# Values of layer 1 for four pairs of heads in one job, with two of its four weight slabs in other tiles, and splits of late outputs placed behind the last transposed weights

## The chip, the cores and the metric

The kernel runs on one core of a Trainium2 chip. The metric is the device time of one execution in microseconds (us); lower is better. The program is one launch: TensorE (PE, with its weight loads as PEld), VectorE (DVE), ScalarE (ACT), GpSimd (POOL) and the DMA queue that SyncE (SP) feeds, each with its own instruction stream that is worked off in order.

## The reference

Two layers of an encoder trunk on 1024 tokens of width 1024, in f32. Every layer does

```
h = rms_norm(x) * (1 + scale(c)) + shift(c);  x = x + gate(c) * mixer(h)
```

and a last `rms_norm` follows. Layer 0's mixer is differential attention beside a bidirectional RG-LRU. Layer 1's mixer, which the change is about, is neighbourhood attention over a 16 x 64 grid:

```
q, k, v, g = split(h @ w_in, 4)                 # 16 heads of 64
p = softmax(q k^T / 8 + relative bias, masked)  # window 8 rows x 16 columns
y = ((p v) * silu(g)) @ w_out
```

## The kernel before, in words

All activations are kept transposed: a tile holds 128 of the 1024 features, and a half `hf` of the tokens (512). A weight matrix comes in slabs of 1024 x 128 (512 KB). `load_next` loads a slab into one of two `raw` tiles by SP's queue. `split_next` cuts it into a high part `whi` (ACT, L187) and a low part `wlo` (POOL, four instructions, L190), both in a format that TensorE multiplies fast. Activations are cut the same way into `ahi` and `alo`. Each product is then three matmuls, high x high, high x low and low x high (`mm3`, L206 to L208). `slab(i)` makes sure that slab i is split, and `ahead(i)` splits it early. Slabs are split in the order of the list `slabs`. The pool and the tags that `split_next` picks say which tile a slab goes into, and a split waits until the last matmul has read the slab that was there before.

`proj` multiplies one slab with half of the tokens: 24 matmuls with 512 columns into one bank of PSUM, then an evacuation, `evac_k`, `evac_q` or `evac_g`. The evacuation of a key (L641 to L644) puts the high part down by ACT (`ks`) and the low part by DVE.

Between layer 0's output and layer 1 lies a boundary stage. Layer 1's input is made from x by a norm: DVE works out the reciprocal root of the mean square in a chain of small instructions on tiles of 128 x 128 (`rstd_rows`, `rs`, `rr`, `rt`, L390 to L396), eight matmuls spread it over all partitions (`bc`, L409), and `make_h` (L416 to L418) makes x * gain * bc on DVE, `ahi` on ACT and `alo` on DVE, for each of eight tiles. The first half of the tokens goes through this while layer 0's second half is still being multiplied. For the second half the PE covers the norm with layer 1's first projections of the first half: k, q and g of pair 0.

Layer 1 works in pairs of heads p = 0 to 7 and 64 units u = 8p + 4hf + b. `na_a` makes a unit's logits (`n`, four matmuls, L673 and L674), DVE adds the bias and takes the maximum (L1383), ACT the exponential (L1386), POOL the division by the sum (L1391). `na_b` transposes the result (`etr`, six matmuls, L1402) and copies it out of PSUM by DVE (L1408) and ACT (L1406). `na_c` multiplies four units with the values (`no`, 48 matmuls, L1420). The PE's time between these is filled from a queue of projections, `Feed`: each step of a job is some six or twelve matmuls and has a price, mostly 1300 ns, and each unit gives a credit, `PUMP1` (4400 ns). `upto` finishes a job by force where a unit needs it.

Values are the one projection with the tokens as the stationary operand. `v1_job(p)` makes them for pairs p and p + 1 from two slabs, for each of eight groups of 128 tokens: 24 matmuls with 256 columns into a bank, then a copy `vt` by ACT or DVE, and a store to the DRAM tensor `vd`. `load_v` reads them back in the layout that `na_c` wants (`vch`).

What sets the order: Python writes the program in the order of these jobs, a scheduler then sorts each engine's instructions by priority and by its own estimate of when each can start, and `high_priority` and `issue_after` move single ones. The resulting order on each engine is fixed.

In layer 1's output stage `out_layer` first splits the eight mixed tiles for both halves (`split_act`, ACT L232 and DVE L233), then runs the output slabs over them in the order of features 6, 0, 1, 2, 3, 4, 5, 7. Pairs from `LATE` = 3 on are gated after their attention (`gate1`, L1319); the output of the last pair is `o_7`.

Of the kernel before, what the change touches and what calls it, by code (L numbers as in the profile page):

```python
# [19 lines left out]
P = 128  # L20
# [9 lines left out]
NW = (3, 3, 7, 3)  # L30
KORDER1 = (6, 0, 1, 2, 3, 4, 5, 7)
PUMP = 745.0
PUMP1 = 4400.0
LATE = 3

DA_HEADS = 4
LRU_CHUNKS = 4
# [60 lines left out]
def kernel(ctx, tc, xT, xTp, small, lamp, adaw, tb, w0, gw, wo0, w1, nab, wo1, out):  # L98
# [62 lines left out]
    def split_next():  # L161
        i = state["split"]
        if i >= len(slabs):
            return
        while state["load"] <= i:
            load_next()
        raw = raws.pop(i)
        pool = wp
        if state["third"] is not None:
            state["turn"] = (state["turn"] + 1) % 3  # L170
            pool = wp if state["turn"] else state["third"]
        tags = ("whi", "wlo")
        if i == 2:
            pool, tags = kqp, ("ks1", "ks1")
        if i == at1["g", 0]:
            pool, tags = mixp[1], ("mix6", "mix7")
        j = i - len(slabs) + KC
        if j >= 0:

            pool = (wp, kqp, mixa, mixp[1])[j // 2]  # L180
            if j >= 2:
                tags = (("ks0", "ks0"), ("ks1", "ks1"), ("mix0", "mix1"), ("mix2", "mix3"),
                        ("mix4", "mix5"), ("mix6", "mix7"))[j - 2]
        hi = pool.tile([P, KC, P], F32R, tag=tags[0], name=f"whi{i}")
        lo = pool.tile([P, KC, P], F32R, tag=tags[1], name=f"wlo{i}")
        with tc.high_priority() if j < 2 else tc.issue_after(state["pool"]):
            A.activation(hi[:], raw[:], AF.Copy)  # L187

            for k in range(0, KC, 2):
                G.tensor_tensor(lo[:, k:k + 2], raw[:, k:k + 2], hi[:, k:k + 2], ALU.subtract)  # L190
# [264 lines left out]
    for p in range(NA_PAIRS):  # L455
        vs = [("v", p), ("v", p + 1)] if p % 2 == 0 else []
        kq = [("k", p), ("q", p)]
        order1 += kq + vs if p else kq + [("g", 0)] + vs
        if 0 < p < LATE:
            order1.append(("g", p))  # L460
    order1 += [("g", p) for p in range(LATE, NA_PAIRS)]
    base1 = {"q": 0, "k": 8, "v": 16, "g": 24}
    for key in order1:
        at1[key] = len(slabs)
# [663 lines left out]
    def out_layer(l, ato, xsrc, xdst, pool, korder, order, view, segments):  # L1128
# [88 lines left out]
    with tc.tile_pool(name="bound", bufs=2) as bp:  # L1217
        make_sel(bp)
        run, tail = out_layer(0, ato0, xTp, x1d, bp, [4, 5, 6, 7, 0, 1, 2, 3], by_fours, by_tile,
                              ((0, 0, 0, HF), (KC, 1, 0, HF)))  # L1220
        r0, r1 = run(0), run(1)
        mod = mods(NM[2], bp, bufs=4, wait=NW[2])
        for c in range(KC):
            some(r0, 1)
            after_dve(mod, 3)

        t0 = tail(0, to_h1)
        for c in range(KC):
# [25 lines left out]
    with ExitStack() as l1:  # L1254
# [9 lines left out]
        def v1_job(p):  # L1264

            i = at1["v", p]
            ws = [slab(i), slab(i + 1)]
            for t in range(8):
                hf, b = divmod(t, 4)
                ps = bank("v1")  # L1270
                for k in range(KC):
                    hi, lo = (t[:, b * P:(b + 1) * P] for t in hact[k, hf])
                    wh, wl = (w[:].rearrange("p (k a) n -> p k (a n)", a=2)[:, k % 4, :]
                              for w in ws[k // 4])
# [3 lines left out]
                vt = ap.tile([P, 256], F32, tag="vt", name="vt", bufs=2)  # L1278
                if t % 2:
                    A.activation(vt[:], ps[:, :256], AF.Copy)  # L1280
                else:
                    V.tensor_copy(vt[:], ps[:, :256])
                state["vd"] = nc.sync.dma_start(
                    vd4[2 * hf:2 * hf + 2, 64 * b:64 * b + 64, P * p:P * p + 256], vt[:]).ins
                if t == 1:
                    ahead(i + 2)
                yield 1300.0

        def load_v(p, b):
# [9 lines left out]

        def load_ahead(p):  # L1300

            if f"1v{p + 1 - (p + 1) % 2}" in feed.done:
                for b in range(4):
                    load_v(p + 1, b)

# [14 lines left out]

        state["gate1"] = gate1
        feed.done.add("1g0")
        for p in range(NA_PAIRS):
            if p:
                feed.add(f"1k{p}", both(at1["k", p], evac_k(("b", p))))
                feed.add(f"1q{p}", both(at1["q", p], evac_q(("b", p))))
            if p % 2 == 0:
                feed.add(f"1v{p}", v1_job(p))
            if 0 < p < LATE:
                feed.add(f"1g{p}", both(at1["g", p], evac_g1l(p)))  # L1330
        for p in range(LATE, NA_PAIRS - 2):
            feed.add(f"1g{p}", both(at1["g", p], evac_g1l(p)))

        def last_gates():

# [59 lines left out]
        def na_b(u, e):  # L1395
# [41 lines left out]
        es, ets = {0: na_a(0)}, {}  # L1437
        for u in range(n_units + 1):

            pump = 1.5 * PUMP1 if u < 3 else PUMP1  # L1440
            if u and u % 4 == 0:
                na_c(u - 4, [ets.pop(u - 4 + b) for b in range(4)])
            if u % 8 == 2:

                p = u // 8
                feed.upto(f"1v{p - p % 2}")
                for b in range(4):
                    load_v(p, b)
            elif u >= 8:
# [51 lines left out]

def _slabs_v(w):

    n = w.shape[1] // 256
    return w.reshape(2, 4, P, n, 256).transpose(3, 0, 2, 1, 4).reshape(2 * n, P, KC, P)


def _t5_bucket(rel):
# [75 lines left out]
```

## Time and profile before

| what | value |
|---|---|
| median of 3 runs | 1181.23 us (1179.83 to 1182.94) |
| the profiled execution | 1183.27 us, of which the span is 1181.5 us |
| PE busy | 1142.2 us, 97% |
| DVE, ACT, POOL busy | 715.9, 559.5, 440.5 us (61%, 47%, 37%) |
| layer 1's units, first logits to last product with values | 618.1 to 1078.4 us |
| value matmuls | 768 with 256 columns |
| matmuls of projections with 512 columns, groups `pp<-ahi` and `pp<-alo` | 3 x 848 |

The page gives the busy time of each engine, the span in 40 slices, the DMA queues, the chain of waits that ended last, and the costliest groups of instructions. A matmul's duration reaches from its issue to its modelled end, and the next begins before that, so the cost of a matmul in a row of them is the distance between two starts. A row of a timeline gives start, duration, engine, line and operation, and in brackets how long the engine was idle before and what ended that.

### The profile page before, as it was taken

The page shows a single profiled execution, that of the slowest core. Times are in us where ns is not written, and L with a number is a line of the kernel's source. Part 1 is how long each engine was busy: PE and PEld are TensorE (multiplying, and loading weights), DVE is VectorE, ACT ScalarE, POOL GpSimd, SP SyncE. Part 2 cuts the span into 40 slices and gives each one's busy share as a digit, 9 for nine tenths or more (in the row PEclk, how much of TensorE's full clock was granted, in tenths as well). Part 3 has the DMA queues.
Part 4 walks back from the last instruction along what each step waited for, and adds up shares of the span by engine and source line. Part 5 has one row for each costly group of instructions (what it writes and reads, how often), then busy time and mean ns, then how long its engine had stood idle before and what let it go on. Part 6 is the DMA issues. An engine that isn't in the chain of part 4 may idle for free.

```text
span 1181.5 us, 19490 instructions
## 1 busy us (share of the span) xinstructions
PE 1142.2 (97%) x7232; PEld 974.7 (82%) x7232; DVE 715.9 (61%) x1422; ACT 559.5 (47%) x1029; POOL 440.5 (37%) x586
## 2 busy tenths in 40 slices
PE   4999999999999999999998999999999999999997
PEld 3788778888887888778788889988988998887896
DVE  6857968699889989768462344334444444454254
ACT  4357685476655557533332444344345444445121
POOL 3135445243343332456522444333243333417200
PEclk8999999999999999999999999999999999999999
DMA  9723141432122012484522533343453543314312
GB/s 330 239 72 123 47 140 56 141 90 79 37 86 64 32 39 72 156 296 173 181 79 91 145 106 98 91 135 110 127 162 99 153 138 106 95 34 149 106 73 72
DMA packets 85791, 136.48 MB, mean 116 GB/s; under 512 B 8000, under 2 KB 49472, under 8 KB 85696
## 3 DMA queue, kind: packets, MB, share of 16 engines
q1 hardware_dynamic: 85696, 135.23, 36.3%
q8 instruction: 57, 0.93, 0.3%
q14 instruction: 38, 0.31, 0.1%
HBM read 112.13 MB, written 16.78 MB: 109 GB/s over the span
## 4 chain that ended last, share of the span: by engine, by line
PE 76%; DVE 9%; DMA 6%; ACT 4%; POOL 2%; issue 1%; SPq 0%; DVEq 0%; ACTq 0%; POOLq 0%
PE pp L206 15%; PE pp L207 15%; PE pp L208 15%; PE no L1420 4%; PE etr L1402 3%; PE v L206 2%; PE v L208 2%; PE v L207 2%; POOL wlo L190 2%; PE atr L1035 2%; PE n L673 2%; DMA ada<-in_adaw_dram 2%; DVE e L1005 2%; PE n L674 2%; PE s L673 1%
## 5 line engine op out<-in xcount | busy, mean ns | idle before, releaser
L206 PE MATMUL pp<-ahi,whi 128*128 128x512 f32 (+1 forms) x976 | 370.1, 379 | 0.1
L207 PE MATMUL pp<-alo,whi 128*128 128x512 f32 (+1 forms) x976 | 368.1, 377 | 0.0
L208 PE MATMUL pp<-ahi,wlo 128*128 128x512 f32 (+1 forms) x976 | 367.6, 377 | 0.2 <-POOL wlo L190 0.2
L190 POOL TENSOR_TENSOR wlo<-raw,whi 128x256 fp32r<-128x256 f32 x320 | 264.3, 859 | 221.0 <-ACT whi L187 199.0
L208 PEld LDWEIGHTS pp<-ahi,wlo 128*128 128x128 f32 x976 | 183.7, 188 | 34.4 <-POOL wlo L190 0.6
L206 PEld LDWEIGHTS pp<-ahi,whi 128*128 128x128 f32 x976 | 183.8, 188 | 32.5 <-issue 0.9
L207 PEld LDWEIGHTS pp<-alo,whi 128*128 128x128 f32 x976 | 183.8, 188 | 30.5 <-issue 0.2
L1391 POOL TENSOR_SCALAR e<-e,r 128x288 f32<-128x288 f32 (+1 forms) x128 | 71.5, 572 | 224.9 <-DVE r L1389 224.8
L187 ACT ACTIVATE whi<-raw 128x1024 fp32r<-128x1024 f32 x80 | 84.3, 1056 | 109.0 <-PE pp L207 58.0
L1386 ACT ACTIVATE e<-e,nm 128x288 f32<-128x288 f32 (+1 forms) x128 | 72.7, 569 | 51.1 <-DVE nm L1383 43.8
L1009 ACT ACTIVATE e<-e,nm 128x1024 f32<-128x1024 f32 x64 | 73.6, 1150 | 46.6 <-DVE nm L1005 46.3
L1408 DVE COPY e<-etr 96x384 f32<-96x384 f32 (+1 forms) x64 | 35.5, 554 | 91.4 <-PE etr L1402 90.4
L1383 DVE CUSTOM_DVE_ANT_0 e<-n,bias 128x288 f32<-128x288 f32 (+1 forms) x128 | 60.5, 504 | 47.8 <-PE n L674 33.0
L1406 ACT ACTIVATE e<-etr 96x384 f32<-96x384 f32 (+1 forms) x64 | 31.3, 490 | 114.9 <-DVE e L1408 111.6
L1005 DVE CUSTOM_DVE_ANT_0 e<-s,tb 128x1024 f32<-128x1024 f32 x64 | 77.3, 1218 | 6.0 <-PE s L674 4.9
L1026 POOL TENSOR_SCALAR e<-e,r 128x256 f32<-128x256 f32 x32 | 33.5, 1046 | 124.4 <-DVE r L1015 76.0
L206 PE MATMUL v<-whi,ahi 128*128 128x256 f32 x256 | 72.8, 284 | 0.0
L208 PE MATMUL v<-whi,alo 128*128 128x256 f32 x256 | 72.5, 283 | 0.0
L207 PE MATMUL v<-wlo,ahi 128*128 128x256 f32 x256 | 72.4, 283 | 0.0
L1042 ACT ACTIVATE ath<-atr 128x512 fp32r<-128x512 f32 x64 | 37.5, 596 | 37.8 <-PE atr L1035 37.5
L1151 DVE SCALAR_TENSOR_TENSOR xh<-pp,mod,xh 128x512 f32<-128x512 f32 (+1 forms) x37 | 23.4, 634 | 49.9 <-PE pp L208 43.3
L1402 PE MATMUL etr<-ident,e 128*96 128x128 f32 (+1 forms) x384 | 52.3, 272 | 0.8 <-POOL e L1391 0.8
(218 smaller groups left out, 2117.0 us busy)
## 6 DMA issues: line engine op xcount, KB each, us to landing
raw<-in_w_dram SPq DMA_DIRECT2D x56, 512.0 KB
ada<-in_adaw_dram SPq DMA_DIRECT2D x96, 256.0 KB
raw<-in_wo_dram SPq DMA_DIRECT2D x24, 512.0 KB
bias<-in_nab_dram SPq DMA_DIRECT2D x64, 144.0 KB
qq<-qq SPq DMA_DIRECT2D x48, 128.0 KB
bias<-in_nab_dram SPq DMA_DIRECT2D x32, 192.0 KB
xT<-in_xT_dram SPq DMA_DIRECT2D x16, 256.0 KB
vd<-vt SPq DMA_DIRECT2D x32, 128.0 KB
```

The source lines that it names most:

```text
L187: A.activation(hi[:], raw[:], AF.Copy)
L190: G.tensor_tensor(lo[:, k:k + 2], raw[:, k:k + 2], hi[:, k:k + 2], ALU.subtract)
L206: T.matmul(ps, lh, rh, start=start, stop=False)
L207: T.matmul(ps, lh, rl, start=False, stop=False)
L208: state["pe"] = T.matmul(ps, ll, rh, start=False, stop=stop).ins
L1005: state["dve"] = V.tensor_tensor_reduce(out=e[:], in0=ps[:].rearrange("p a b -> p (a b)"), in1=tbt["tb"][:, o:o + S], scale=-1.0, scalar=3 ...
L1009: A.activation(e[:], e[:], AF.Exp, scale=-1.0, bias=nm[:], accum_out=sums[:, m:m + 1])
L1383: state["dve"] = V.tensor_tensor_reduce(out=e[:, m, :n], in0=ps[:, m, :n], in1=bias["now"][m][:, :n], scale=-1.0, scalar=3.0e38, op0=ALU.a ...
L1386: A.activation(e[:, m, :n], e[:, m, :n], AF.Exp, scale=-1.0, bias=nm[:, m:m + 1], accum_out=sums[:, m:m + 1])
L1391: state["pool"] = G.tensor_scalar(e[:, m, :n], e[:, m, :n], r[:, m:m + 1], 0.0, ALU.mult, ALU.add).ins
L1402: T.transpose(pt[:kn, m, j * P:(j + 1) * P], e[:, m, j * kn:(j + 1) * kn], ident[:])
L1420: T.matmul(po[64 * m:64 * m + 64, b * P:(b + 1) * P], vch[p, b][:kn, j + hf, 64 * m:64 * m + 64], ets[b][:kn, m, j * P:(j + 1) * P], start ...
```

## The change

It has five parts.

1. `v1_job` makes the values of four pairs at once from four slabs. A slab holds 256 of the features of h for 512 columns, and a group of tokens takes 24 matmuls with 512 columns. It pauses three times inside a group, not once, and copies a bank out in two pieces of 256 columns, one by DVE and one by ACT, each with its store. There are two such jobs, `v0` and `v4`, where there were four.
2. Homes: of the first job's slabs, the first two are split into the tiles of the later mixed outputs 4 and 5, and 2 and 3; of the second job's, the last two into those of 4 and 5, and 6 and 7.
3. All four slabs of the first job are split ahead in the boundary stage.
4. The order of jobs is written out in `JOBS1`. The credit of a unit is 5000 ns up to unit 30 and 3450 ns behind it, and doubled for unit 0.
5. The splits of the mixed tiles 3 and up in layer 1's output stage are placed behind DVE's last copy of transposed weights, and the modulation that layer 1's output needs is spread over the units from 17 on, not from 26.

```diff
-PUMP1 = 4400.0
+PUMP1 = (5000.0, 3450.0)
+JOBS1 = "k0 q0 g0 v0 k1 q1 g1 k2 q2 g2 k3 q3 v4 k4 q4 k5 q5 k6 q6 g3 k7 q7 g4 g5 g6 g7"
...
+        pool, tags = wp, ("whi", "wlo")
+        if i == 2:
+            pool, tags = kqp, ("ks1", "ks1")
+        elif i == at1["g", 0] or i == at1["v", 4] + 3:
+            pool, tags = mixp[1], ("mix6", "mix7")
+        elif i in (at1["v", 0], at1["v", 4] + 2):
+
+            pool, tags = mixp[1], ("mix4", "mix5")
+        elif i == at1["v", 0] + 1:
+            pool, tags = mixa, ("mix2", "mix3")
+        elif state["third"] is not None:
...
-                    split_act(k, hf, mixed[k][:, hf * HF:(hf + 1) * HF], V, order)
+
+                    with tc.issue_after(state["etr"]) if l and k >= LATE else nullcontext():
+                        split_act(k, hf, mixed[k][:, hf * HF:(hf + 1) * HF], V, order)
...
-        ahead(at1["g", 0] + 2)
+        for j in range(2, 5):
+            ahead(at1["g", 0] + j)
...
-            ws = [slab(i), slab(i + 1)]
+            ws = [slab(i + j) for j in range(4)]
...
-                for k in range(KC):
+                for n, k in enumerate(range(KC)):
...
-                    mm3(ps[:, :256], hi, lo, wh, wl, k == 0, k == KC - 1)
-                    if k == 3:
+                    mm3(ps, hi, lo, wh, wl, n == 0, n == KC - 1)
+                    if n % 2 == 1 and n < KC - 1:
                         yield 1300.0
...
+                for j in range(2):
+                    vt = ap.tile([P, 256], F32, tag="vt", name="vt", bufs=2)
+                    src, c0 = ps[:, 256 * j:256 * j + 256], P * p + 256 * j
+                    if j:
+                        A.activation(vt[:], src, AF.Copy)
+                    else:
+                        V.tensor_copy(vt[:], src)
+                    state["vd"] = nc.sync.dma_start(
+                        vd4[2 * hf:2 * hf + 2, 64 * b:64 * b + 64, c0:c0 + 256], vt[:]).ins
...
-                    V.tensor_copy(e[:kn, m, :], pt[:kn, m, :384])
+                    state["etr"] = V.tensor_copy(e[:kn, m, :], pt[:kn, m, :384]).ins
...
-            pump = 1.5 * PUMP1 if u < 3 else PUMP1
+            pump = PUMP1[u > 30] * (2.0 if u == 0 else 1.5 if u < 3 else 1.0)
...
-            if u >= 26:
+            if u >= 17:
```

The engines' orders are the same up to the boundary stage. There ACT's order changes. `whi_5828` and `whi_5769` are the slabs of g and q of pair 0, `ks_5803` and `ks_5804` the evacuation of its keys, `qq` that of its queries, `ahi_1` the second half of layer 1's input. Before:

```order
L187 ACTIVATE whi_5828<-raw_5767 128x1024
L187 ACTIVATE whi_5769<-raw_5728 128x1024
L1156 ACTIVATE sq<-xh_1_7_5689 128x512
L641 ACTIVATE ks_5803<-pp_0_5778 64x4x2x64
L642 ACTIVATE ks_5804<-pp_0_5778 64x4x2x64
L657 ACTIVATE qq_5862<-pp_0_5837 64x512
L658 ACTIVATE qq_5863<-pp_0_5837 64x512
L417 ACTIVATE ahi_1_5886<-xh_1_0_5369,mod_102 128x512
```

And in the changed kernel:

```order
L192 ACTIVATE whi_5828<-raw_5767 128x1024
L192 ACTIVATE whi_5769<-raw_5728 128x1024
L1159 ACTIVATE sq<-xh_1_7_5689 128x512
L192 ACTIVATE whi_6014<-raw_5776 128x1024
L644 ACTIVATE ks_5803<-pp_0_5778 64x4x2x64
L645 ACTIVATE ks_5804<-pp_0_5778 64x4x2x64
L192 ACTIVATE whi_6051<-raw_5835 128x1024
L660 ACTIVATE qq_5862<-pp_0_5837 64x512
L661 ACTIVATE qq_5863<-pp_0_5837 64x512
L422 ACTIVATE ahi_1_5886<-xh_1_0_5369,mod_102 128x512
```

The splits of the first two value slabs, `whi_6014` and `whi_6051`, now stand ahead of the keys' evacuation and of the queries'; in the kernel before they stand behind all eight `ahi_1`.

DVE's order at the same place, where `rs`, `rr` and `rt` are the chain of the second half's norm. Before:

```order
L390 TENSOR_SCALAR rs<-ssl_1_5809 128x128
L391 TENSOR_SCALAR rr<-rs 128x128
L394 SCALAR_TENSOR_TENSOR rt<-rr 128x128
L643 TENSOR_TENSOR ks_5803<-pp_0_5778,ks_5803 64x4x2x64
L644 TENSOR_TENSOR ks_5804<-pp_0_5778,ks_5804 64x4x2x64
L395 TENSOR_TENSOR rt<-rt,rs 128x128
L396 SCALAR_TENSOR_TENSOR rr<-rt,rr 128x128
```

And in the changed kernel:

```order
L395 TENSOR_SCALAR rs<-ssl_1_5809 128x128
L396 TENSOR_SCALAR rr<-rs 128x128
L399 SCALAR_TENSOR_TENSOR rt<-rr 128x128
L400 TENSOR_TENSOR rt<-rt,rs 128x128
L401 SCALAR_TENSOR_TENSOR rr<-rt,rr 128x128
L646 TENSOR_TENSOR ks_5803<-pp_0_5778,ks_5803 64x4x2x64
L647 TENSOR_TENSOR ks_5804<-pp_0_5778,ks_5804 64x4x2x64
```

In both kernels the keys' low part stands inside the chain. It was ahead of the chain's last eight instructions, and is now ahead of the last six.

The third place is the end of the units, on DVE. `e<-etr` are the copies of the last two units' transposed weights, `alo_0` and `alo_1` the splits of the mixed tiles of the two halves. Before:

```order
L233 TENSOR_TENSOR alo_1_10958<-sg_2_7616,ahi_1_10957 128x512
L233 TENSOR_TENSOR alo_1_10962<-o_3_8335,ahi_1_10961 128x512
L233 TENSOR_TENSOR alo_1_10966<-o_4_8974,ahi_1_10965 128x512
L233 TENSOR_TENSOR alo_1_10970<-o_5_9586,ahi_1_10969 128x512
L1408 COPY e<-etr_10859 128x384
L1408 COPY e<-etr_10868 96x384
L679 SCALAR_TENSOR_TENSOR sg_10856<-sg_10856,pp_1_10831 128x512
L233 TENSOR_TENSOR alo_1_10946<-o_6_10187,ahi_1_10945 128x512
L1319 SCALAR_TENSOR_TENSOR o_7_10705<-o_7_10705,sg_10856 128x512
L233 TENSOR_TENSOR alo_1_10974<-o_7_10705,ahi_1_10973 128x512
```

And in the changed kernel:

```order
L1413 COPY e<-etr_10444 128x384
L238 TENSOR_TENSOR alo_1_10558<-sg_2_7212,ahi_1_10557 128x512
L1413 COPY e<-etr_10468 96x384
L238 TENSOR_TENSOR alo_0_10514<-o_6_9842,ahi_0_10513 128x512
L682 SCALAR_TENSOR_TENSOR sg_10465<-sg_10465,pp_1_10431 128x512
L238 TENSOR_TENSOR alo_0_10530<-o_3_8317,ahi_0_10529 128x512
L238 TENSOR_TENSOR alo_0_10534<-o_4_8861,ahi_0_10533 128x512
L238 TENSOR_TENSOR alo_0_10538<-o_5_9369,ahi_0_10537 128x512
L1327 SCALAR_TENSOR_TENSOR o_7_10305<-o_7_10305,sg_10465 128x512
L238 TENSOR_TENSOR alo_0_10542<-o_7_10305,ahi_0_10541 128x512
```

The first half's late splits (`alo_0` of 6, 3, 4, 5 and 7), which stood ahead of the last unit's logits, now follow the last copy, and that of tile 7 follows `o_7`'s second gate. On ACT `o_7`'s evacuation, which that gate needs, has a split of an output slab (`whi_10689`) ahead of it; before, it had none behind the last copy:

```order
L192 ACTIVATE whi_10609<-raw_10227 128x1024
L681 ACTIVATE sg_10465<-pp_1_10431 128x512
L1411 ACTIVATE e<-etr_10468 96x384
L192 ACTIVATE whi_10689<-raw_10616 128x1024
L1432 ACTIVATE o_7_10305<-no_10477 128x512
```

`whi_10609`, the second output slab, likewise stands ahead of ACT's last copy, as two such splits did before.

More of the change, by code (lines that the diff above doesn't have):

```diff
@@ L167, in split_next @@
         raw = raws.pop(i)
-        pool = wp
-        if state["third"] is not None:
+        pool, tags = wp, ("whi", "wlo")
[8 more added lines that the diff above has]
+        elif state["third"] is not None:
             state["turn"] = (state["turn"] + 1) % 3
             pool = wp if state["turn"] else state["third"]
[L172 to L176, printed above, removed]
         j = i - len(slabs) + KC
@@ L454 @@
     order1 = []
[L455 to L461, printed above, removed]
+    for key in JOBS1.split():
+        key = key[0], int(key[1])
+        order1 += [key] if key[0] != "v" else [("v", key[1] + j) for j in range(4)]
     base1 = {"q": 0, "k": 8, "v": 16, "g": 24}
@@ L1270, in v1_job @@
                 ps = bank("v1")
-                for k in range(KC):
+                for n, k in enumerate(range(KC)):
                     hi, lo = (t[:, b * P:(b + 1) * P] for t in hact[k, hf])
-                    wh, wl = (w[:].rearrange("p (k a) n -> p k (a n)", a=2)[:, k % 4, :]
-                              for w in ws[k // 4])
-                    mm3(ps[:, :256], hi, lo, wh, wl, k == 0, k == KC - 1)
-                    if k == 3:
+                    wh, wl = (w[:].rearrange("p (k a) n -> p k (a n)", a=4)[:, k % 2, :]
+                              for w in ws[k // 2])
+                    mm3(ps, hi, lo, wh, wl, n == 0, n == KC - 1)
+                    if n % 2 == 1 and n < KC - 1:
                         yield 1300.0
[L1278 to L1284, printed above, removed]
+                for j in range(2):
[7 more added lines that the diff above has]
+                        vd4[2 * hf:2 * hf + 2, 64 * b:64 * b + 64, c0:c0 + 256], vt[:]).ins
                 if t == 1:
-                    ahead(i + 2)
+                    ahead(i + 4)
                 yield 1300.0
@@ L1300, in load_ahead @@
         def load_ahead(p):
-            if f"1v{p + 1 - (p + 1) % 2}" in feed.done:
+            if f"1v{p + 1 - (p + 1) % 4}" in feed.done:
                 for b in range(4):
@@ L1322 @@
         feed.done.add("1g0")
[L1323 to L1332, printed above, removed]
+        for job in JOBS1.split()[3:-2]:
+            kind, p = job[0], int(job[1])
+            evac = {"k": evac_k, "q": evac_q}.get(kind)
+            if kind == "v":
+                feed.add("1" + job, v1_job(p))
+            else:
+                feed.add("1" + job, both(at1[kind, p], evac(("b", p)) if evac else evac_g1l(p)))
         def last_gates():
@@ L1445 @@
                 p = u // 8
-                feed.upto(f"1v{p - p % 2}")
+                feed.upto(f"1v{p - p % 4}")
                 for b in range(4):
@@ L1502, in _slabs_v @@
 def _slabs_v(w):
-    n = w.shape[1] // 256
-    return w.reshape(2, 4, P, n, 256).transpose(3, 0, 2, 1, 4).reshape(2 * n, P, KC, P)
+    n = w.shape[1] // HF
+    return w.reshape(4, 2, P, n, HF).transpose(3, 0, 2, 1, 4).reshape(4 * n, P, KC, P)
 def _t5_bucket(rel):
```

## The prediction

> **What bounds the kernel now.** First the page: who is busy, and who stands in the chain of waits.
>
> ```profile
> PE 1142.2 (97%) x7232; PEld 974.7 (82%) x7232; DVE 715.9 (61%) x1422; ACT 559.5 (47%) x1029; POOL 440.5 (37%) x586
> PE 76%; DVE 9%; DMA 6%; ACT 4%; POOL 2%; issue 1%; SPq 0%; DVEq 0%; ACTq 0%; POOLq 0%
> ```
>
> TensorE is the bound, and among the units it is so without a gap, as one stretch of the table of windows shows (first PE, then PEld, DVE, ACT and POOL; near the end the clock, the DMA share and GB/s):
>
> ```profile
> 750.00:800.00 50.00, 50.00 (x319) 43.88 (x318) 17.08 (x48) 19.97 (x46) 20.93 (x34) 1.00 0.41 124
> ```
>
> So matmul time taken from the units is time gained, and a wait only counts where TensorE runs into it. The groups of matmuls give durations of 284 ns with 256 columns and 393 ns with 512:
>
> ```profile
> L206 PE MATMUL v<-whi,ahi 128*128 128x256 f32 x256 | 72.8, 284 | 0.0
> L206 PE MATMUL pp<-ahi,whi 128*128 128x512 f32 x848 | 333.5, 393 | 0.1
> ```
>
> These overlap, so I take the price from starts in the timeline: two value matmuls 20 apart, and two of a projection 80 apart.
>
> ```profile
> 639.79 0.28 PE L206 MATMUL v<-whi,ahi 128*128 128x256 f32 x1
> 642.19 0.28 PE L208 MATMUL v<-whi,alo 128*128 128x256 f32 x1
> ...
> 599.73 0.39 PE L206 MATMUL pp<-ahi,whi 128*128 128x512 f32 x1
> 617.87 0.39 PE L208 MATMUL pp<-ahi,wlo 128*128 128x512 f32 x1
> ```
>
> 2.40 / 20 is 120 ns with 256 columns, 18.14 / 80 is 227 ns with 512.
>
> **Term 1, the value matmuls.** 768 x 0.120 = 92.2 us become 384 x 0.227 = 87.2 us: 5.0 us less. Between units a start costs up to 0.229, which gives 4.3. I take **-4.7**. The 32 copies and 32 stores of 256 columns stay as many; a bank now holds 5.5 us of work, not 2.9, so they have more time. Credits change only which step lies in which unit: every unit keeps at least two steps between its logits and its transposes.
>
> By the Trainium skill ("TensorE: Matmul & The Clock Gate", "Wait — 56ns, not 53.3ns?") a warm matmul starts N / 2.4 GHz + 2.5 ns behind the last, 109 and 216 ns; the term would be an estimated -0.9 us. The rows have 11 ns more per start in both, and the gain is nearly all in that.
>
> **Term 2, a new wait in the boundary stage.** The orders show ACT's `whi_6014` now ahead of the keys' evacuation. What happens there before (SPq is SP's DMA queue):
>
> ```profile
> 585.12 2.01 ACT L187 ACTIVATE whi<-raw 128x1024 fp32r<-128x1024 f32 x2 [6.36 <-DMA raw<-in_w_dram]
> 586.26 6.09 POOL L190 TENSOR_TENSOR wlo<-raw,whi 128x256 fp32r<-128x256 f32 x8 [4.66 <-ACT whi L187]
> 588.15 0.59 ACT L641 ACTIVATE ks<-pp 64x512 fp32r<-64x512 f32 x1 [0.50 <-PE pp L208]
> 589.55 3.15 SPq L158 DMA_DIRECT2D raw<-in_w_dram  x2
> 591.09 0.68 DVE L643 TENSOR_TENSOR ks<-pp,ks 64x512 fp32r<-64x512 f32 x1
> 594.79 0.29 DVE L396 SCALAR_TENSOR_TENSOR rr<-rt,rr 128x128 f32<-128x128 f32 x1
> 595.40 1.05 PE L409 MATMUL bc<-rr,sel 128*128 128x128 f32 x8
> ```
>
> The raw slab of `whi_6014` is the one issued at 589.55, once POOL had freed its tile; nothing ahead of it changes. How long such a load takes stands in the chain:
>
> ```profile
> 581.63 3.47 DMA raw<-in_w_dram
> ...
> 1070.23 3.49 DMA raw<-in_wo_dram
> ```
>
> So `whi_6014` cannot start before 589.55 + 3.5 = 593.05. The keys' evacuation, at 588.15 before, follows it at 594.1 (the next ACT instruction starts about 1.0 behind). DVE's `ks_5803`, at 591.09 before, starts at 594.7, and its second part ends at 596.1 (2 x 0.69). Six instructions of the norm's chain are queued behind it. And POOL, idle here before, is then at work on the two slabs' low parts: from 594.2 to about 600 (8 x 0.7 to 0.86). What DVE's chain costs beside such work shows in the first half's norm:
>
> ```profile
> 543.37 2.93 POOL L190 TENSOR_TENSOR wlo<-raw,whi 128x256 fp32r<-128x256 f32 x4 [1.49 <-ACT whi L187]
> 543.43 0.77 DVE L391 TENSOR_SCALAR rr<-rs 128x128 int32<-128x128 int32 x1
> 545.74 0.71 DVE L396 SCALAR_TENSOR_TENSOR rr<-rt,rr 128x128 f32<-128x128 f32 x1
> 546.49 0.29 DVE L394 SCALAR_TENSOR_TENSOR rt<-rr 128x128 f32<-128x128 f32 x1
> ```
>
> Beside POOL four in a row take 0.71 to 0.77, alone 0.29. Six take 6 x 0.33 = 2.0 or 6 x 0.75 = 4.5, and `bc`, which TensorE was ready for at 595.40, starts at 598.2 or at 600.5. In TensorE's order the next projection (g) stands behind `bc`, so it idles 2.8 to 5.1 us. All six meet POOL, so I take **+4.9**. What is late next is `ahi` and `alo` of the second half, which follow `bc` as before and move with it; the queries' copies by DMA, now behind two more slab loads on SP, have until the first logits, some 20 us. Nothing gives the time back.
>
> **Term 3, the clock.** After the one gap of this size among the later stages, TensorE ran at half speed:
>
> ```profile
> 622.55 0.44 PE L673 MATMUL n<-ks,qq 128*128 128x384 f32 x1 [2.81 <-DVE sg L679]
> 623.77 0.42 PE L206 MATMUL v<-whi,ahi 128*128 128x256 f32 x1
> 626.12 0.41 PE L208 MATMUL v<-whi,alo 128*128 128x256 f32 x1
> ...
> 619.00:628.00 9.00, 6.19 (x38) 0.81 0.52 170
> ```
>
> Eleven starts in 2.35 us, 214 ns for 120; a granted clock of 0.81 over 9 us is 1.7 us lost. I add **+1.7** for the new gap, 0 if it passes, 3.4 if two such stretches follow.
>
> The Trainium skill ("TensorE: Matmul & The Clock Gate", "Part 1: The HAM clock gate") says that half rate comes after a whole idle window of about 3.4 us that runs free; 2.8 us would not reach it. By that the term would be 0 for the shorter gap. The trace shows the drop after 2.81.
>
> The gap at 622.55 itself stays: its chain (a split that waits for TensorE's last use of k's slab, POOL, a load, a split, then g's gate) is the same with other slabs in it. Eight more starts' worth of value work ahead of it is 0.2 us more: -0.2.
>
> **Term 4, two old waits.** The second unit's logits came late because of a bias:
>
> ```profile
> 633.71 0.56 DVE L1383 CUSTOM_DVE_ANT_0 e<-n,bias 128x384 f32<-128x384 f32 x1 [3.73 <-DMA bias<-in_nab_dram]
> 634.33 0.44 PE L673 MATMUL n<-ks,qq 128*128 128x384 f32 x1 [0.97 <-DVE nm L1383]
> ```
>
> TensorE now has 43 value matmuls of 0.227 there, 9.8 us, for 64 of 0.120, 7.7: 2.1 us later, wait gone, **-1.0**. And at the end of the units:
>
> ```profile
> 1071.52 2.82 POOL L1391 TENSOR_SCALAR e<-e,r 128x288 f32<-128x288 f32 x2 [1.32 <-DVE r L1389]
> 1074.39 0.53 PE L1402 MATMUL etr<-ident,e 128*96 128x128 f32 x3 [0.78 <-POOL e L1391]
> ```
>
> POOL waited for `r`, which stood behind `alo` on DVE. With those moved away, that is -0.8, with ACT's copy up to -1.2. Against it stands the new order there: `o_7`'s evacuation waits behind `whi_10689`. Its load follows POOL's last division and one low part (2.9): with 3.5 for the load, 1.06 for the split, 0.6 for the evacuation, 0.7 to 1.06 for the gate and 0.7 to 1.0 for `alo` of tile 7, this is 0.3 to 1.2 us behind TensorE, which comes to tile 7 about 8.4 us after the last g projection. I take **-0.4** for both, from -1.2 to +0.8.
>
> The second value job's four slabs come in time: from the end of k3, which frees the last home, TensorE has some 18 us of projection and unit work, and POOL one low part of three to go. If that cover is gone, each late slab costs its load and split, some 7 us.
>
> **Sum:** -4.7 + 4.9 + 1.7 - 0.2 - 1.0 - 0.4 = +0.3. The profiled execution took 1183.27 us, 1.8 of it outside its span; it becomes 1183.6. The median of the runs is 2.0 below that execution, so I forecast **1181.5 us**, no change. What a measurement can tell here is 0.3%, 3.5 us.
>
> **The rivals.**
>
> *The boundary wait is not paid.* Were the keys' evacuation not held, or the chain short enough to end by 595.4, only terms 1 and 4 would stay: -4.7 - 0.2 - 1.0 - 0.4 = -6.3, 1175 us. The order of the rows speaks against it. Half of it can be: a gap of 2.8 with no loss of clock gives -4.7 + 2.8 - 1.6 = -3.5, 1177.7, just faster. Together 26%, of which 12% the whole.
>
> *Slower, by the tail.* One mechanism: `whi_10689` ahead of `o_7`. Loads of output slabs also take longer:
>
> ```profile
> 508.03 5.58 DMA raw<-in_wo_dram
> ```
>
> With 5.6 for the load the stall before tile 7 is 0.8 + 2.1 = 2.9 us, enough for the loss of clock: 2.1 + 1.7 on top of the sum, 1181.5 + 3.8 = 1185.3 us. It decides from about 5 us of loading on. 14%.
>
> *Columns alone cost.* If two starts with 256 columns cost no more than one with 512, term 1 is 0 to -0.9: 1185 to 1186 us. 120 against 227 in the rows speaks against it. 3%. The Trainium skill's spacing ("TensorE: Matmul & The Clock Gate", as above) comes near to this.
>
> *The durations are the price.* 768 x 0.284 - 384 x 0.393 = 67 us, 1114 us. The starts exclude it; 1%.
>
> The forecast and its own range, 1178 to 1184.5, keep 56%.
>
> **Range and chances.** The range of 1175 to 1185.5 takes in the lower bounds of terms 2 and 3 (1177.7), the case without the wait (1175) and the tail (1185.3). Faster by over 0.3% is below 1177.7: the first rival and the last, 27%. Slower is above 1184.8: the tail, columns alone, 17%. Within it: 56%.
>
> **What would show it.** Value matmuls 227 ns apart, 384 of them. On ACT the split of a value slab ending near 594 with the DMA named ahead of it, the keys' evacuation right behind. The chain `rt`, `rr` at 0.7 beside POOL, and `bc` at 598 to 600.5 with a gap ahead of it that DVE ended; the granted clock below 1 in the 10 us behind. No wait of a second at the third unit's logits. In the output stage a gap of up to 1 us before tile 7. I am wrong if `bc` stands at 595.4, if the load lands ahead of the keys, or if TensorE shows gaps among the units at the second value job.

## The result and the profile after

The change made the kernel slower: 1192.97 us (median of 6 runs, 1190.49 to 1194.41) against 1182.65 us for the kernel before on the same chip (6 runs, 1179.83 to 1184.55). The ratio is 1.0088, 95% interval 1.0075 to 1.0101. The forecast was 1181.5 us and no change, with a range of 1175 to 1185.5; the time lies above all of it.

The profiled execution took 1190.49 us, with a span of 1188.8, and is 7.2 longer than the profiled one before (1183.27). First the page's busy times and its chain of waits:

```profile
PE 1142.2 (96%) x6848; PEld 956.4 (80%) x6848; DVE 715.6 (60%) x1422; ACT 560.0 (47%) x1029; POOL 442.8 (37%) x586
PE 37%; DMA 5%; ACT 2%; issue 1%; DVE 1%; POOL 1%; SPq 0%; DVEq 0%; ACTq 0%; POOLq 0%
```

TensorE executes 384 matmuls fewer and is busy as long as before; the busy time of overlapping matmuls says little. Nor can the chain's 37% be held against the 76% before: its shares add up to 47%, because in this execution the chain starts only at 627.79 us, behind the boundary stage. What TensorE lost is read from the gaps.

The boundary stage, on ACT:

```profile
584.32 2.01 ACT L192 ACTIVATE whi<-raw 128x1024 fp32r<-128x1024 f32 x2 [6.29 <-DMA raw<-in_w_dram]
592.48 1.06 ACT L192 ACTIVATE whi<-raw 128x1024 fp32r<-128x1024 f32 x1 [5.63 <-DMA raw<-in_w_dram]
593.45 0.57 ACT L644 ACTIVATE ks<-pp 64x512 fp32r<-64x512 f32 x1
```

The split of the first value slab waits 5.63 us for its load, and the keys' evacuation, at 588.15 before, follows at 593.45. On DVE the chain of the norm is queued behind the keys' low part, beside POOL's low parts of the value slabs (POOL is at work from 593.62 to 599.34):

```profile
595.36 0.69 DVE L647 TENSOR_TENSOR ks<-pp,ks 64x512 fp32r<-64x512 f32 x1
596.09 0.48 DVE L399 SCALAR_TENSOR_TENSOR rt<-rr 128x128 f32<-128x128 f32 x1
596.61 0.70 DVE L400 TENSOR_TENSOR rt<-rt,rs 128x128 f32<-128x128 f32 x1
599.52 0.29 DVE L401 SCALAR_TENSOR_TENSOR rr<-rt,rr 128x128 f32<-128x128 f32 x1
```

```profile
593.62 5.72 POOL L195 TENSOR_TENSOR wlo<-raw,whi 128x256 fp32r<-128x256 f32 x8 [2.02 <-ACT whi L192]
```

TensorE's rows with a gap of more than 2 us behind 50 us are three (the number in brackets is the idle time before the row, and what ended it):

```profile
599.96 0.86 PE L414 MATMUL bc<-rr,sel 128*128 128x128 f32 x3 [5.21 <-DVE rr L401]
...
628.56 0.44 PE L676 MATMUL n<-ks,qq 128*128 128x384 f32 x1 [2.37 <-DVE sg L682]
...
783.75 0.94 PE L1425 MATMUL no<-e,vc 96*64 96x128 f32 x10 [2.78 <-ACT e L1411]
```

The first is the new wait that the prediction works out, the second the old one. The third was not foreseen. It stands in the middle of the 48 matmuls of `no`, among the units, and ACT's rows there show why:

```profile
777.40 0.19 ACT L1391 ACTIVATION_READ_ACCUMULATOR e<-e,nm 128x1 f32 x1
780.10 2.00 ACT L192 ACTIVATE whi<-raw 128x1024 fp32r<-128x1024 f32 x2 [2.51 <-DMA raw<-in_w_dram]
782.01 0.57 ACT L644 ACTIVATE ks<-pp 64x512 fp32r<-64x512 f32 x1
782.59 0.59 ACT L645 ACTIVATE ks<-pp 64x512 fp32r<-64x512 f32 x1
783.21 0.49 ACT L1411 ACTIVATE e<-etr 96x384 f32<-96x384 f32 x1
```

`whi` x2 are two slabs of the second value job. One of the two `raw` tiles is held by the other slab of that row, so the loads come one at a time, and SP issues this one when POOL is done with the slab ahead of it:

```profile
774.00 2.85 POOL L195 TENSOR_TENSOR wlo<-raw,whi 128x256 fp32r<-128x256 f32 x4 [3.48 <-ACT whi L192]
776.87 0.33 SPq L159 DMA_DIRECT2D raw<-in_w_dram  x1
```

ACT waits 2.51 us for it, then cuts two slabs and evacuates keys, and only then copies the transposed weights that TensorE's last ten matmuls of `no` need.

What follows the two larger gaps, in the table of windows (length, PE busy, granted clock, DMA share, GB/s):

```profile
593.26:596.67 3.41, 1.49 (x7) 1.00 0.29 117
596.67:600.09 3.42, 0.13 (x1) 1.00 0.49 153
600.09:603.50 3.41, 3.41 (x13) 0.50 0.78 229
603.50:606.91 3.41, 3.41 (x17) 1.00 0.01 2
```

3.41 us at half clock, so 1.7 us lost; the same after 784.41. Behind the old gap at 628.56 the clock stayed at 1.00 in this execution, where it had dropped before.

By the gaps and the starts, the profiled execution's 7.2 us are these, beside the prediction's terms:

| place | predicted | measured |
|---|---|---|
| value matmuls (sum of their starts, 91.3 to 87.9 between two kernels without the waits, below) | -4.7 | -3.4 |
| gap ahead of `bc` | +4.9 | +5.2 |
| half clock behind it | +1.7 | +1.7 |
| old gap (2.81 to 2.37), and the half clock behind it gone here | -0.2 | -0.4, -1.7 |
| third unit's logits (0.97, gone) | -1.0 | -1.0 |
| end of the units (0.86 before tile 7, 0.63 and 0.23 for ACT's copies; 0.78 and 0.06 gone) | -0.4 | +0.9 |
| second value job: gap of 2.78 and half clock | 0 | +4.5 |
| `no` near 692 (0.41 and 0.15) | 0 | +0.6 |
| sum | +0.3 | +6.4 |

0.8 us in small differences is left over. The small gaps near 692 come about in the same way as the large one: ACT waits in a split for a load, behind it stand the keys' evacuation, DVE's low part of the keys and then DVE's copy of transposed weights, for which TensorE waits.

```profile
688.46 1.06 ACT L192 ACTIVATE whi<-raw 128x1024 fp32r<-128x1024 f32 x1 [2.66 <-DMA raw<-in_w_dram]
692.67 1.45 PE L1425 MATMUL no<-e,vc 96*64 96x128 f32 x12 [0.41 <-DVE e L1413]
```

### The profile page after: what moved, and what is told of

Same layout as the page of the kernel before. It is cut to its first block, busy times and chain, and to the rows that moved or that the text cites. A ratio compares the mean times of both kernels' runs of the same rounds, so it can differ in the third digit from the quotient of the medians.

```text
span 1188.8 us, 18722 instructions
## 1 busy us (share of the span) xinstructions
PE 1142.2 (96%) x6848; PEld 956.4 (80%) x6848; DVE 715.6 (60%) x1422; ACT 560.0 (47%) x1029; POOL 442.8 (37%) x586
## 5 line engine op out<-in xcount | busy, mean ns | idle before, releaser
L195 POOL TENSOR_TENSOR wlo<-raw,whi 128x256 fp32r<-128x256 f32 x320 | 268.2, 870 | 237.3 <-ACT whi L192 202.8
L1407 PEld LDWEIGHTS etr<-ident,e 128*96 128x96 f32 (+1 forms) x384 | 44.7, 133 | 9.9 <-issue 1.0
L676 PE MATMUL s<-ks,qq 128*128 128x512 f32 x128 | 52.3, 409 | 0.2 <-DVE nm L1008 0.2
L351 DVE SCALAR_TENSOR_TENSOR macc<-ada,ctmp,macc 128x512 f32<-128x512 f32 x56 | 47.0, 839 | 8.9 <-DMA ada<-in_adaw_dram 8.5
```

What stands on the lines that cost most here:

```text
L676: T.matmul(dst, qsel(q[m]), k, start=True, stop=False)
L1407: T.transpose(pt[:kn, m, j * P:(j + 1) * P], e[:, m, j * kn:(j + 1) * kn], ident[:])
```

## The experiments

Theory A: time is lost where ACT, which works in order, waits in a weight's split for a DMA while a copy that TensorE needs stands behind it. The rival, B: the new order of jobs and credits costs among the units, and a gap that is removed uncovers the next wait. All kernels but one are the changed kernel with the edit shown. `behind` names the ACT instruction that a split is queued after:

```diff
+        with tc.issue_after(behind) if behind is not None else nullcontext():
+            with tc.high_priority() if j < 2 else tc.issue_after(state["pool"]):
+                A.activation(hi[:], raw[:], AF.Copy)
```

Runs of one group share their runs of the kernel before (1182.5, 1180.8 and 1182.1 us in the three groups), so ratios to it are what is compared between groups; 0.001 is 1.2 us.

**keys_first**

```diff
+        if i in (at1["v", 0], at1["v", 0] + 1):
+            behind = state["ks" if i == at1["v", 0] else "qq"]
```

> The splits of the first two value slabs are put behind the first half's evacuations of the keys and of the queries on ACT; all else is as in the change. Theory A, held evacuations: the change loses its time where ACT, which works in order, waits for a DMA in a split while a copy that TensorE needs stands behind it. Then bc is back at about 595.4 to 596 (one or two of the chain's steps still beside POOL), its gap of 5.21 us falls below 1, the granted clock stays 1.00 around 600 to 604, and the time falls by 5.2 + 1.7 less at most 1, that is by 6 to 7 us, to about 1186.5 from 1193. Theory B, the schedule: the loss lies in the new order of jobs and credits among the units, and the gap at bc hides a later one: then the second half's chain or the first value job waits instead and the time falls by 2 us or less.

Measured: 1183.93 us, ratio 1.0002 (0.9992 to 1.0012). The gap ahead of `bc` is gone and the clock is whole:

```profile
593.24 1.13 PE L419 MATMUL bc<-rr,sel 128*128 128x128 f32 x8
```

```profile
600.00:604.00 4.00, 4.00 (x20) 3.30 (x19) 3.91 (x7) 1.90 (x4) 0.00 (x0) 1.00 0.31 117
```

The size is above the 6 to 7 us expected: 9.0 us between the medians. Theory B's 2 us is excluded for this place.

**copy_first**

```diff
+        if i == at1["v", 4] + 3:
+            behind = state["acopy"][15]    # ACT's copy of the transposes of unit 15
```

> The split of the second value job's last slab is put behind ACT's copy of the transposes of unit 15; all else is as in the change. Theory A: the gap of 2.78 us ahead of the last ten matmuls of 'no' at 783.75 goes and with it the 3.41 us at half clock behind it: 2.8 + 1.7 = 4.5 us less, about 1188.5. The second value job starts on TensorE some 20 us later, so the slab, now split one or two units later, still comes in time. Theory B: the wait moves to the job's start, near 800, as its last slab is late, and the time falls by 1 us or not at all.

Measured: 1186.14 us, ratio 1.0030 (1.0021 to 1.0039), 6.8 us less than the change, where 4.5 were expected; the spans of the two profiled executions differ by 4.0 (1188.8 to 1184.8). Where the rest comes from is not shown. The copy now stands ahead of the split that held it, and the 48 matmuls of `no` run without a break:

```profile
780.95 0.49 ACT L1416 ACTIVATE e<-etr 96x384 f32<-96x384 f32 x1
781.34 1.05 ACT L196 ACTIVATE whi<-raw 128x1024 fp32r<-128x1024 f32 x1
```

```profile
779.57 2.84 PE L1431 MATMUL no<-e,vc 96*64 96x128 f32 x48
```

Nor is TensorE's work late at the job's start near 800, where theory B expected it. The small gaps at 692 are gone in this trace too, though nothing was changed there. Of the seven traces of the changed kernel and its variants that have the old gap, the five without a half clock behind it show a gap there (0.35 to 0.77 us), and the two with one, this and part5_undone, show none. ACT's split waits for its load in all of them, 2.60 to 3.02 us in the five, 1.78 and 1.84 in the two.

**three_first**: both edits and a third.

```diff
+        if i == at1["k", 1]:
+            behind = state["sg"]
```

> Both edits, and the split of the slab behind the first value job (k of pair 1) put behind the second half's gate evacuation, which removes the wait of DVE's sg ahead of the first unit's logits (2.81 before, 2.37 with the change). Theory A: 6.5 + 4.5 + 2.4, and 1.7 more in those executions in which the clock drops after the 2.4: 13.4 to 15 us less than the change, 1178 to 1179.5, that is 3 to 4.5 us below the kernel before. Theory B: the first unit's logits wait for something else (the queries' copies by DMA, the first unit's bias) and the units keep their extra time: 1184 to 1188.

Measured: 1175.30 us, ratio 0.9935 (0.9923 to 0.9948), 17.7 us less than the change and faster than the kernel before. Its spans differ by 14.1 (1188.8 to 1174.7); the three gaps, the 692 ones and the two stretches of half clock in the changed kernel's trace make 5.2 + 2.8 + 2.4 + 0.6 + 2 x 1.7 = 14.4. The stretches that had the gaps are full:

```profile
600.00:650.00 50.00, 50.00 (x231) 41.69 (x230) 20.58 (x43) 17.44 (x34) 13.62 (x21) 1.00 0.31 101
...
750.00:800.00 50.00, 50.00 (x309) 42.37 (x309) 20.00 (x57) 22.66 (x51) 23.49 (x38) 1.00 0.47 142
```

**gate_first**: the third edit alone.

> The change, with only the split of the slab behind the first value job put behind the second half's gate evacuation. If the three waits are separate faults whose prices add up, the gap of 2.37 us at the first unit's logits goes, with half a stretch of 1.7 on the average, and nothing else moves: 2.4 to 4.1 us less than the change, a ratio to the kernel before of 1.0053 to 1.0068 against 1.0088. If what it frees is taken back by the next wait (the small gaps at 692, which the traces show only where no half clock fell behind 628), 1 us or less is left: 1.0080 or more.

Measured: 1188.59 us, ratio 1.0053 (1.0041 to 1.0066), at the upper end of what separate prices give. Singly the three edits take 0.0086, 0.0058 and 0.0035 off the ratio, 0.0179 in sum, and together 0.0153: separate, as far as these intervals can tell.

**before_gate_first**: the same edit in the kernel before.

> The kernel before, with one edit: the split of the slab behind the first value job is put behind the second half's gate evacuation on ACT. If the old gap of 2.81 us at the first unit's logits was the same fault (an evacuation held by a split that waits for its load), it goes, and with it the half clock behind it: 2.8 + 1.7 = 4.5 less, about 1178. It also says what the change is worth between kernels without such stalls: three_first at 1175.3 should then stand about 4.7 + 1.0 - 0.8 = 4.9 below this one by the terms of the prediction, which would put this one at 1180; if it comes out at 1176 or below, the four-pair value jobs gain nothing.

Measured: 1177.92 us, ratio 0.9967 (0.9955 to 0.9980): 2.9 us less by the medians and 3.9 by the ratio, for 4.5 expected. In its trace the gap at the first unit's logits is gone, and no half clock follows there. So the old gap was the same fault, and it was there to be taken without the change. Between kernels without such waits the change is worth 0.9935 / 0.9967 = 0.9968, 3.8 us (by the two intervals, some 2 us either way). By starts, the value matmuls take 91.3 us in this kernel (768) and 87.9 in three_first (384): 3.4 us, not 4.7. The mean start is 119 ns with 256 columns here, where the rows quoted in the prediction gave 120, and 229 with 512, where projections gave 227.

**part5_undone**

```diff
-                    with tc.issue_after(state["etr"]) if l and k >= LATE else nullcontext():
-                        split_act(k, hf, mixed[k][:, hf * HF:(hf + 1) * HF], V, order)
+                    split_act(k, hf, mixed[k][:, hf * HF:(hf + 1) * HF], V, order)
...
-            if u >= 17:
+            if u >= 26:
```

> Only the last part of the change is undone: the splits of the late outputs are no longer queued behind the copies of the last units, and the steps of the last modulation start at unit 26 again, not 17. Theory A: this part moves less than 1 us: the wait of 0.86 before tile 7 goes, a wait for POOL's division of about 0.8 comes back: 1192 to 1194. Theory B: the modulation's loads and DVE steps among units 17 to 26, where TensorE loses some 2 us more than before in small gaps, are part of the loss: 1190 to 1191.

Measured: 1191.34 us, ratio 1.0065 (1.0052 to 1.0078). In its trace the wait before tile 7 is gone and the wait for POOL's division did not come back; ACT's copies cost 0.35 and 0.22 there, for 0.63 and 0.23 in the change.

**three_p5undone**: this together with three_first's edits.

> The three held copies freed and the last part of the change undone together. part5_undone alone was 1.6 below the change. If that came from its own place (the wait before tile 7, the modulation among the units) it is had here as well: 1173.7. If it came from another execution's clock, the time stays at 1175.3 within 0.6.

Measured: 1174.95 us, ratio 0.9944 (0.9930 to 0.9959), against 0.9935 without it. The last part of the change is worth nothing that these runs can tell on top of the three edits; what it does alone (1.6 us between medians, with intervals that overlap) stays open, and is small.

**warm**: the price of the clock alone.

```diff
+        for _ in range(warm):    # 5 for the first half's queries
+            mm3(ps, wh[:, ks[0], :], wl[:, ks[0], :], hact[ks[0], hf][0][:],
+                hact[ks[0], hf][1][:], True, True)
```

> The change, with fifteen more matmuls of 512 columns (3.4 us, their result is overwritten) ahead of the first half's projection of the queries, so that TensorE works through most of the time in which it waits for bc. It should wait only about 1.8 us for bc, which stays at about 600, since DVE's chain does not depend on this projection. Theory A: the gap itself costs nothing more, but the half clock behind it goes: 1.7 us less than the change for one stretch of 3.41, 3.4 for two: 1189.6 to 1191.3. If the clock has no share in the loss, the time stays at 1193; if bc's chain does hang on the projection, it is 1196.

Measured: 1189.90 us, ratio 1.0071 (1.0057 to 1.0085), against 1.0088: 2 us less, as theory A has it, though the intervals overlap. `bc` comes when it came before, after a shorter gap, and the clock behind it is whole:

```profile
599.95 1.13 PE L417 MATMUL bc<-rr,sel 128*128 128x128 f32 x8 [2.21 <-DVE rr L404]
```

```profile
600.00:604.00 4.00, 4.00 (x22) 3.44 (x23) 2.81 (x5) 0.72 (x1) 0.00 (x0) 1.00 0.63 197
```

The mean granted clock is 0.991 to 0.994 in its five executions and 0.986 to 0.992 in the change's six. So the wait itself costs what `bc` is late, and the loss of clock is a second price, which useless work avoided here.

**second_late** and **pool_clear**: POOL's share in the wait for `bc`. Both leave the first slab's split ahead of the keys.

```diff
+        if i == at1["v", 0] + 1:
+            behind = state["qq"]      # second_late
...
+            behind = state["ahi1"]    # pool_clear: the second half's first ahi, behind bc
```

> Only the second value slab's split is put behind the queries' evacuation; the first stays ahead of the keys, so the keys' evacuation is as late as in the change (593.5). What differs is POOL: the second slab's low part, which ran beside the end of DVE's chain from 596.5 to 599.3, is gone from there. By the prediction's price (0.72 beside POOL, 0.29 alone) four of the six steps lose 0.4 each: bc at about 598.2 instead of 599.96, a gap of 3.5, 1.7 us less: 1191. If DVE's steps are slow there for another reason, bc stays at 600 and the time at 1193.

Measured: 1191.04 us, ratio 1.0082 (1.0069 to 1.0095); the gap is 4.97, not the 3.5 expected. The split moved by only about 1 us, and POOL was idle from 597.21 to 597.81, in which time two steps of the chain fell:

```profile
597.39 0.29 DVE L405 TENSOR_TENSOR rt<-rt,rs 128x128 f32<-128x128 f32 x1
597.72 0.29 DVE L406 SCALAR_TENSOR_TENSOR rr<-rt,rr 128x128 f32<-128x128 f32 x1
598.04 0.70 DVE L404 SCALAR_TENSOR_TENSOR rt<-rr 128x128 f32<-128x128 f32 x1
```

```profile
594.41 2.80 POOL L200 TENSOR_TENSOR wlo<-raw,whi 128x256 fp32r<-128x256 f32 x4 [2.20 <-ACT whi L196]
597.81 2.97 POOL L200 TENSOR_TENSOR wlo<-raw,whi 128x256 fp32r<-128x256 f32 x4 [0.60 <-ACT whi L196]
```

Three of the six were slow, not two: the experiment was too weak, and its reading of DVE right. The stronger one:

> The change, with the second value slab's split on ACT put behind the first ahi of the second half, which itself follows bc. The first slab's split stays ahead of the keys, so these are as late as in the change. On POOL only the first slab's low part (2.8 us from about 594.4) is left beside DVE's chain; the second follows bc. If the steps are slow exactly while POOL works (0.69 against 0.29), only the first one or two of the six stay slow, bc comes 1.2 to 1.6 us earlier than in the change in relation to the end of the keys' evacuation, the gap falls from 5.21 to 3.6 to 4.0, and the time by 1.2 to 1.6 us against the change. If the steps are slow for another reason (the keys' split before them, the clock), the gap stays above 4.7 and the time within 0.6.

Measured: 1189.69 us, ratio 1.0065 (1.0050 to 1.0079), gap 3.46. POOL's low part ended at 595.42, and all five steps behind that take 0.29:

```profile
595.10 0.48 DVE L404 SCALAR_TENSOR_TENSOR rt<-rr 128x128 f32<-128x128 f32 x1
595.61 0.29 DVE L405 TENSOR_TENSOR rt<-rt,rs 128x128 f32<-128x128 f32 x1
...
596.91 0.29 DVE L406 SCALAR_TENSOR_TENSOR rr<-rt,rr 128x128 f32<-128x128 f32 x1
```

From the end of the keys' low part to `bc` it is 597.35 - 595.06 = 2.29 us, against 599.96 - 596.05 = 3.91 in the change: POOL's share of the wait is 1.6 us, and the held keys are the rest.

By the Trainium skill ("SBUF — State Buffer", "Who interferes with whom") DVE and GpSimd share a pair of ports under an exclusive lock, and a DVE instruction with two inputs in SBUF contends with a GpSimd instruction that reads SBUF. The traces agree: a DVE step of the chain that is wholly beside POOL takes 0.69 to 0.72, as long as one of POOL's four (2.80 / 4 = 0.70).

**three_pump**: three_first with the credits of the kernel before.

```diff
-PUMP1 = (5000.0, 3450.0)
+PUMP1 = (4400.0, 4400.0)
...
-            pump = PUMP1[u > 30] * (2.0 if u == 0 else 1.5 if u < 3 else 1.0)
+            pump = PUMP1[u > 30] * (1.5 if u < 3 else 1.0)
```

> three_first, with the credits of the kernel before (4400 per unit, 1.5 times that in the first three) in place of 5000, 3450 and the double first. Theory A: credits only say which step stands in which unit, TensorE is never short of steps, and the time stays within 1 us of three_first: a ratio to the kernel before of 0.993 to 0.9945. Theory B in its weaker form, that the change's credits cost or save something by themselves among the units: below 0.992 or above 0.9955, with gaps ahead of the transposes or of the logits that three_first does not have.

Measured: 1198.15 us, ratio 1.0134 (1.0118 to 1.0150): 23 us slower than three_first, and far outside what theory A expected. Late units have no projection between logits and transposes, and their products with the values are broken up:

```profile
985.49 0.44 PE L1439 MATMUL no<-e,vc 96*64 96x128 f32 x4
985.86 0.40 PE L689 MATMUL n<-ks,qq 128*128 128x288 f32 x1
...
986.60 0.66 PE L1439 MATMUL no<-e,vc 96*64 96x128 f32 x8
989.23 1.51 PE L1420 MATMUL etr<-ident,e 128*128 128x128 f32 x6 [1.97 <-POOL e L1409]
```

In one piece, a block of 48 takes 2.77 us in three_first, from its first start to the start of what follows; here eight take 2.63, of which 1.97 is the wait behind them. By starts, waits included, `no` takes 59.0 us in place of 45.8. Among the units TensorE has thirteen gaps of over 0.15 us, 9.7 us in all, against three with 1.4 in three_first; the rest of the loss is in smaller pieces. So the change's credits belong to its order of jobs, and one cannot be judged without the other. This does not put a part of the slowdown on the credits that the change has: with them the units are full.

## Why the prediction was wrong

**Term 1** had the right mechanism and was too large by 1.3 us: 3.4 against 4.7. It was sized from two short rows, the one for 512 columns a projection's: 120 and 227 ns, where the sums over all value matmuls give 119 and 229.

**Term 2** held step by step. `whi_6014` started at 592.48 (predicted from 593.05), the keys' evacuation at 593.45 (594.1), the chain was lengthened beside POOL (the first step in part, four steps in full, the last not, where all six were taken), and the gap is 5.21 (4.9). keys_first shows that the order on ACT causes it, pool_clear that 1.6 us of it are POOL's.

**Term 3** was right in kind, and short for most executions. In the traces of copy_first, part5_undone and gate_first, which have the same wait for `bc`, the half clock behind it lasts 6.83 us, two stretches and not one as in those of the change and of second_late; in the first two it also comes behind the old gap, where the changed kernel's own trace has none. That fits a median 2.5 us above the profiled execution, and the 9.0 us of keys_first where 6 to 7 were expected. The granted clocks of the change's six executions go the same way: 0.989 and 0.992 in the two of 1190.5 us, 0.986 to 0.988 in the four of 1192.9 to 1194.4. Where the clock was lost in executions without a trace is not shown.

**Term 4**'s first half was right (the third unit's wait is gone); its second half came out 1.3 us worse than taken, just outside its range. The rival by the tail did not come to pass: the gap before tile 7 is 0.86.

**The step that failed** first of all is the cost of nothing for the second value job: "The second value job's four slabs come in time". They did come in time for the job, which runs from 800 without a gap. But the cover was looked for at the matmuls that use the slabs, and not at what is queued behind their splits on ACT. The free homes let the scheduler put two of these splits early; the two `raw` tiles, which stay as few, then make ACT wait in them. The prediction had found this very fault in the boundary stage and did not look for it at the second place where the same edit was made. It cost 2.8 us and 1.7 of clock in the trace, and 6.8 between medians by copy_first. Alone it does not account for the whole miss: without it the kernel takes 1186.14 us, still just above the range.

The sum was +0.3 by the working; against the profiled execution it failed by 6.9 us, of which the second job makes 4.5, term 1 and the end of the units 1.3 each, and the old gap's clock -1.7 the other way. The median then stood 2.5 above the profiled execution, where 2.0 below had been taken from three executions of the kernel before. This failed as well: a difference between executions, carried over from one kernel to another, makes 4.5 of the 11.5 us between forecast and median, as much as the second value job in the trace; the clock of term 3 probably has a share in it. The last of the signs named ("I am wrong if ... TensorE shows gaps among the units at the second value job") is what happened.

## What to carry to other kernels

An early split, load or copy is only free if everything behind it on its engine's queue may wait as long as it does: for each instruction that a change lets move ahead, list what stands behind it and who waits for that, at every place where the edit applies. More homes for results do not help while the tiles that the loads go into stay few; that more of these would help was not tried. Here queueing such splits, at three places, behind the copies that they held was worth 1.5%, the change itself 0.3%.

## What the runs showed of the hardware

The clock drops by windows. In all traces the stretches at half clock start and end on a grid of 3.41 us, whose phase differs between executions (in the change 19.83, 40.31, 600.09 and 784.41: 6, 164 and 54 steps apart). Whether the clock drops goes with how much TensorE worked in the window just over. Three windows and the one behind each, one fence for each kernel (length, PE busy with its count, granted clock, DMA share, GB/s):

```profile
627.39:630.81 3.42, 2.25 (x11) 1.00 0.03 13
630.81:634.22 3.41, 3.41 (x17) 1.00 0.85 294
```

```profile
625.94:629.36 3.42, 1.44 (x7) 1.00 0.52 165
629.36:632.77 3.41, 3.41 (x10) 0.50 0.42 143
```

```profile
618.03:621.44 3.41, 1.59 (x8) 1.00 0.22 79
621.44:624.85 3.41, 3.41 (x17) 1.00 0.73 240
```

The first is the change's old gap of 2.37 us, cut in two by the grid (2.21 and 2.25 busy): no drop. The second is copy_first's of 1.98, all in one window with 1.44 busy: a drop. The third is keys_first's of 1.99, with 1.59 busy: none. gate_first dropped after a window with 1.77 busy. So a gap of 2 us costs another 1.7, or nothing, by its phase; behind the gaps of over 1.2 us among these traces it never dropped with 2.0 or more of 3.41 us busy, always with 1.44 or less, and between the two both are seen.

Whether a second window follows at half clock goes the same way. In copy_first the wait for `bc` reached into the first one:

```profile
598.64:602.05 3.41, 2.73 (x11) 0.50 0.68 209
602.05:605.46 3.41, 3.41 (x10) 0.50 0.09 22
```

In the four stretches of two windows the first had 2.16 to 2.81 us busy (copy_first, gate_first, part5_undone at `bc`; keys_first at 775.05). Behind gaps of over 1.2 us, the stretches of one window had 2.9 or more.

The Trainium skill ("TensorE: Matmul & The Clock Gate", "Part 1: The HAM clock gate") has the free-running window of about 3.4 us, and the traces agree with that. It has the half rate come after a whole idle window; here a window that was idle for 58% of its time (1.98 of 3.41) was enough.
